# One decoder layer with mLSTM and differential attention: a new hand-written order of steps, norms as steps of their own, and a merge in pairs

## The chip, the cores and the metric

The kernel runs on one core of a Trainium2 chip. The metric is the device time of one execution in microseconds. All matrix products run on the matmul engine (TensorE, PE in the profile); VectorE (DVE), ScalarE (ACT) and GpSimd (POOL) do the rest, and most transfers are issued from SyncE's queue (SP).

## The reference

One layer over 512 tokens of width 1024 in float32:

```python
h = rmsnorm(x, norm_mix_g)
proj = h @ w_in        # mLSTM q,k,v,o,i,f | attention q,k,v | two branch gates
qk = silu(causal_dwconv(concat([mq, mk]), m_conv_w, m_conv_b))     # width 4
hm = mlstm_chunkwise(mq_c, mk_c, mv, i_pre, f_pre)                 # 4 heads x 128
ya = (sigmoid(mo) * head_rmsnorm(hm, m_norm_g)) @ w_br_m
a  = softmax(q1 k1^T/8 + bias) - lam * softmax(q2 k2^T/8 + bias)   # 4 heads, causal
yb = (head_rmsnorm(a @ dv, da_norm_g) * (1 - lam_init)) @ w_br_d
x  = x + (sigmoid(g_a) * ya + sigmoid(g_b) * yb) @ w_out
u  = causal_dwconv(rmsnorm(x, norm_ffn_g) @ w_up, ffn_conv_w, ffn_conv_b)   # width 3
x  = x + (gelu(gate) * value) @ w_down                             # d_ff 2816
x  = x + sigmoid(rmsnorm(x, norm_ple_g) @ w_ple_gate) * (p @ w_ple)
return rmsnorm(x, norm_final_g)
```

## The kernel before

Activations are kept with features on the 128 partitions and the 512 tokens along the free axis, so x is eight tiles of 128x512. To keep float32 accuracy each operand of a product is split into a high and a low part (`split`: ScalarE copies the high part, VectorE subtracts it), and `mm3` (L94) makes three matmuls of each product, on lines 96, 97 and 98; so helpers' lines stand in the profile, and the tile's name says whose step it is. `wload` (L100) brings 128x1024 weights by SP into `raw`, and splits them into `whi` and `wlo`; each of the three has two buffers. One weight tile feeds 24 matmuls of 512 columns.

PSUM has eight banks of 128x512: four under the tag "mm" for projections, two "sc" for scores, sums and transposes, two "acc" for the products of a head (`num` and `den` of an mLSTM head, `av` of an attention head). SBUF tags with few buffers are "ev" (3: `u` and `y` of a convolution, `y` of an attention query or key), "rb" (3), "e" (4), "hn" (4), "qk" (10), "hz" (16), "v" (16: values of both branches, later the mixed chunks) and "x" (8: the branch gates).

The mixing stage is written as a list of steps, `ORDER` (L49). A planner goes through the steps' instructions in this order as priorities and fixes, when the program is built, the sequence of each engine from modelled durations; it draws later steps forward where an earlier one is not ready in its model. Weight loads and their splits have a raised priority. On the chip each engine works through its sequence in order. The steps:

- `mqN`, `mkN` (`conv_silu`, L213): projection, four-tap convolution on VectorE, SiLU by Tanh. The projection's bank is read by one VectorE multiplication (L219).
- `if0`, `ct0`: the gates' projection and their scans on VectorE.
- `mN` (`mlstm`, L409): four score products, weighted products into `num` and `den`.
- `MN` (`mlstm_end`, L432): the sum of squares and the output gate with its projection; `NN` (`mlstm_norm`, L450): the root by Ln and Exp (`rsqrt_of`, L152), which need another table of ScalarE than Tanh, and the split into `hmh`, `hml`.
- `dqN`, `dkN`, `dv0` (L240, L251, L281): attention's queries, keys and values. `dv0` is 96 matmuls into all four "mm" banks at once.
- `bias0`: bias tiles by GpSimd's queue, tied behind the last convolution's memset traced so far.
- `aN` (`attention`, L459): eight score tiles with a softmax each (VectorE adds the bias and takes the maximum, L472; a negation, L475; Exp on ScalarE, L476; a reciprocal, L477; L480 and L481 combine the two halves), transposes (`at`) and the product with the values (`av`).
- `AN` (`attention_end`, L491): square, sum over features, root, split into `hdh`, `hdl`.
- `gaN`, `gbN` (`gate`, L502): branch gates.

After the list comes the merge (L549 to L565), chunk by chunk: chunk j takes one weight tile, whose first half multiplies the four mLSTM heads into `ya` and whose second half the four attention heads into `yb`; the gates' Tanh is tied behind `last_exp`, the Exp of the last norm. The output projection (`wo`), the ConvFFN (`ug`, `uv`, `wd`) and the embedding (`pg`) follow and are untouched.

Of the kernel before, what the change touches and what calls it, by code (L numbers as in the profile page):

```python
# [11 lines left out]
F32 = mybir.dt.float32  # L12
# [34 lines left out]


ORDER = """  # L49
if0 mq0 mk0 mq1 mk1 ct0 m0 m1 mk3 mq2 dk0 M0 M1 mk2 bias0 m2 mq3 M2 m3 dq0 dv0 M3 a0 dk1 dq1  # L50
A0 a1 N0 A1 dk2 dq2 N1 ga3 dq3 a2 N2 A2 ga0 ga2 gb1 dk3 N3 a3 gb3 gb2 gb0 ga1 A3
"""


# [1 line left out]
def trunk_kernel(ctx, tc, xT, pT, par, biasT, lamv, w_if, w_in, w_v, w_br, w_out, w_up,  # L56
# [12 lines left out]
    def rt(tag, name):  # L69
        return big.tile([P, S], F32R, tag=tag, name=name, bufs=NBUF[tag])  # L70
# [76 lines left out]
            nc.scalar.activation(q, src, AF.Square)  # L147
            nc.vector.tensor_add(acc, acc, q)

    last_exp = None  # L150

    def rsqrt_of(r, v, a, before=None):  # L152

        if before is not None:
            with tc.issue_after(before.ins):
                nc.scalar.preload_act_table_set("natural_log_exp_and_others")
        nc.scalar.activation(r, v, AF.Ln, scale=2.0 ** -LN_SHIFT)
        nonlocal last_exp
        last_exp = nc.scalar.activation(r, r, AF.Exp, scale=-0.5, bias=lnb)
        nc.scalar.activation(a, r, AF.Square)  # L160
        nc.vector.scalar_tensor_tensor(a, v, -0.5, a, op0=ALU.mult, op1=ALU.mult)
        nc.vector.scalar_tensor_tensor(r, a, 1.5, r, op0=ALU.add, op1=ALU.mult)
# [293 lines left out]
        return hi, lo  # L456


    def attention(hh, q, k):  # L459
        av = []  # L460
        for i in range(NB):
            n = (i + 1) * P
            nw = max(n, 2 * P)
            es, sums = [], []
            for z in range(2):
                s = ps("sc", f"ds{hh}{i}{z}", nw)
                for b in range(2):
                    nc.tensor.matmul(s, lhsT=q[z][:, i * P:(i + 1) * P], rhs=k[z][b][:, :nw],  # L468
                                     start=b == 0, stop=b == 1)
                e = tt("e" if z == 0 else "rb", f"e{z}", n)  # L470
                mx = tp.tile([P, 4], F32, tag="mx", name="mx", bufs=8)
                nc.vector.tensor_tensor_reduce(  # L472
                    out=e, in0=s[:, :n], in1=bias[hh][:, S - n:], scale=1.0, scalar=-3.0e38,
                    op0=ALU.add, op1=ALU.max, accum_out=mx[:, 0:1])
                nc.vector.tensor_scalar_mul(mx[:, 1:2], mx[:, 0:1], -1.0)  # L475
                nc.scalar.activation(e, e, AF.Exp, bias=mx[:, 1:2], accum_out=mx[:, 2:3])  # L476
                nc.vector.reciprocal(mx[:, 3:4], mx[:, 2:3])  # L477
                es.append(e)
                sums.append(mx[:, 3:4])
            nc.vector.tensor_scalar(es[1], es[1], sums[1], nlam, op0=ALU.mult, op1=ALU.mult)  # L480
            nc.vector.scalar_tensor_tensor(es[0], es[0], sums[0], es[1], op0=ALU.mult, op1=ALU.add)  # L481
            av.append(es[0])
        o = ps("acc", f"av{hh}")
        for j in range(NB):
            tps = ps("sc", f"at{hh}{j}", S - j * P)
            for i in range(j, NB):
                nc.tensor.transpose(tps[:, (i - j) * P:(i - j + 1) * P], av[i][:, j * P:(j + 1) * P], ident)
            weighted("a", j, lambda a, b: split(a, b, tps), dv, hh, (o,))
        return o

    def attention_end(hh, o):  # L491
        y, v, r = tt("hn", "y"), tt("hn", "v"), tt("hn", "r")
        nc.scalar.activation(y, o, AF.Copy, scale=col(C_GD + hh))
        ss, last = mean_square(o, v, f"hd{hh}")
        nc.vector.tensor_scalar(v, ss, 1.0 / P, EPS, op0=ALU.mult, op1=ALU.add)
        rsqrt_of(r, v, ss, None if hh else last)
        nc.vector.tensor_mul(y, y, r)
        hi, lo = rt("hz", f"hdh{hh}"), rt("hz", f"hdl{hh}")
        split(hi, lo, y, 1.0 - LAM_INIT)
        return hi, lo  # L500

    def gate(c, name):  # L502
# [9 lines left out]
    for step in ORDER.split():  # L512
        what, i = step[:-1], int(step[-1])
        if what == "if":
            rd, cols = gates()
        elif what == "ct":
            ct = turn_cols(cols)
        elif what == "mq":
            mq[i] = conv_silu(i, 0.5, f"mq{i}")
        elif what == "mk":  # L520
            mk[i] = conv_silu(4 + i, 0.5 * P ** -0.5, f"mk{i}")
        elif what == "mo":
            mo[i] = out_gate(i)
        elif what == "m":
            sums[i] = mlstm(i)
        elif what == "M":
            hm[i] = mlstm_end(i, *sums[i], mo.get(i))
        elif what == "N":
            hm[i] = mlstm_norm(i, *hm[i])
        elif what == "dv":  # L530
            dv = vproj(1, "dv")
        elif what == "bias":
            bias, nlam = make_bias(), make_nlam()
        elif what == "dq":
            dq[i] = queries(8 + i, f"dq{i}")
        elif what == "dk":
            dk[i] = keys(12 + i, f"dk{i}")
        elif what == "a":
            sums[i] = attention(i, dq[i], dk[i])
        elif what == "A":  # L540
            hd[i] = attention_end(i, sums[i])
        elif what == "ga":
            ga[i] = gate(20 + i, "ga")
        elif what == "gb":
            gb[i] = gate(28 + i, "gb")
    hm, hd = ([t[i] for i in range(H)] for t in (hm, hd))


    mixed = []  # L549
    for j in range(KD):  # L550
        ta = ga[j] if j in ga else gate(20 + j, "ga")
        tb = gb[j] if j in gb else gate(28 + j, "gb")
        with tc.issue_after(last_exp.ins):
            for t in (ta, tb):
                nc.scalar.activation(t, t, AF.Tanh, scale=0.5)
        w = wload(w_br[j])
        oa, ob = ps("mm", "ya"), ps("mm", "yb")
        proj(oa, w, 0, hm)
        proj(ob, w, 4, hd)
        nc.vector.scalar_tensor_tensor(ta, ta, 1.0, oa, op0=ALU.add, op1=ALU.mult)  # L560
        nc.vector.scalar_tensor_tensor(tb, tb, 1.0, ob, op0=ALU.add, op1=ALU.mult)
        nc.vector.tensor_add(ta, ta, tb)
        hi, lo = rt("v", f"mxh{j}"), rt("v", f"mxl{j}")
        split(hi, lo, ta, 0.5)
        mixed.append((hi, lo))  # L565


    x2, h2 = [], []
# [238 lines left out]
def _pack(x, p, rel_bias, norm_mix_g, w_in, b_if, m_conv_w, m_conv_b, m_norm_g, da_lambda, da_norm_g,  # L807
          w_br_m, w_br_d, w_out, norm_ffn_g, w_up, ffn_conv_w, ffn_conv_b, w_down, norm_ple_g,
          w_ple_gate, w_ple, norm_final_g):
    w = w_in[0]  # L810
    mq, mk, mv, mo = (w[:, 512 * i:512 * (i + 1)] for i in range(4))
    gif = np.zeros((D, 64), np.float32)
    gif[:, 0:H] = w[:, 2048:2052]
    gif[:, 32:32 + H] = w[:, 2052:2056]
    dq, dk, dv = (w[:, 2056 + 512 * i:2056 + 512 * (i + 1)] for i in range(3))
    win = np.concatenate([mq, mk, dq, dk, mo, w[:, 3592:]], axis=1)
    wv = np.concatenate([v.reshape(4, 2, P, S).transpose(0, 2, 1, 3).reshape(4, P, 2 * S) for v in (mv, dv)])
    nf = DFF // P
    order = np.stack([nf + np.arange(nf), np.arange(nf)], axis=1).ravel()
    wup = _chunks(w_up[0])[order]  # L820
    par = np.zeros((P, NPAR), np.float32)
    for c, v in ((C_GMIX, norm_mix_g[0]), (C_GFFN, norm_ffn_g[0]), (C_GPLE, norm_ple_g[0]),
                 (C_GM, m_norm_g[0]), (C_GD, da_norm_g[0])):
        v = _cols(v)
        par[:, c:c + v.shape[1]] = v
    mc = np.concatenate([m_conv_w[0], m_conv_b], axis=0)
    par[:, C_MCONV:C_MCONV + 40] = mc.reshape(5, 8, P).transpose(2, 1, 0).reshape(P, 40)
    fc = np.concatenate([ffn_conv_w[0], ffn_conv_b], axis=0)
    par[:, C_FCONV:C_FCONV + 176] = fc.reshape(4, 2 * nf, P)[:, order].transpose(2, 1, 0).reshape(P, 176)
    par[0:H, C_B] = b_if[0, :H]  # L830
    par[32:32 + H, C_B] = b_if[0, H:]
    return {
        "xT": _fmajor(x[0]), "pT": _fmajor(p[0, 0]), "par": par, "biasT": _bias_tiles(rel_bias),
        "lamv": da_lambda[0],
        "w_if": gif.reshape(KD, P, 64).transpose(1, 0, 2).reshape(P, KD * 64), "w_in": _chunks(win), "w_v": wv,
        "w_br": np.concatenate([_chunks(w_br_m[0]), _chunks(w_br_d[0])], axis=2),
        "w_out": _chunks(w_out[0]), "w_up": wup, "w_down": _chunks(w_down[0]),
        "w_gate": w_ple_gate[0].reshape(KD, P, D), "w_ple": w_ple[0].reshape(2, P, 2, S).transpose(2, 1, 0, 3).reshape(2, P, D), "gfin": norm_final_g[None],
    }
# [18 lines left out]
```

## Time and profile before

| | us |
|---|---|
| median of 3 runs | 837.1 (836.33 to 837.5) |
| the profiled execution | 836.26 |
| its span, first to last instruction | 833.3 |

TensorE is busy in nearly the whole span and the other engines are not. Its mean granted clock is 0.992 of full speed. By stage: the value projection of the mLSTM branch to 30 us, the steps of the list to about 273, the merge and the output projection to about 408, the ConvFFN to about 780, the embedding and the last norm to the end. Idle time of another engine costs nothing by itself; what counts is where TensorE waits, for whom, and at which clock it runs.

### The profile page before, as it was taken

Reading aid. Unit: us, or ns where it says so; the run is one execution under the profiler, and the core shown is the slowest. Engines: PE = TensorE matmul, PEld = TensorE weight load, DVE = VectorE, ACT = ScalarE, POOL = GpSimd, SP = SyncE. Lnnn points to the kernel's source line nnn. Section 1 sums busy time; section 2 is a strip of 40 time slices with the busy share of each in tenths; the row PEclk is TensorE's granted clock in tenths of the full one; section 3 lists DMA queues with packets and bytes.
Section 4 is the critical chain, followed back from the end, with each engine's and each line's share of the span. In section 5 each row is a group of like instructions: output and inputs, shape, how many; then the busy total and the mean of one; then the engine's idle time right before and its main releaser. Section 6 shows DMA issues by size and latency. Waiting matters only on the chain.

```text
span 833.3 us, 9859 instructions
## 1 busy us (share of the span) xinstructions
PE 811.2 (97%) x3661; PEld 665.4 (80%) x3661; DVE 539.7 (65%) x873; ACT 397.8 (48%) x614; POOL 27.3 (3%) x111
## 2 busy tenths in 40 slices
PE   8999999999999699999999999999999999999995
PEld 6878878878777588888788888888888888888884
DVE  7689885589977654455677777777777333343545
ACT  6546854487664632334554444444444432232434
POOL 0011200000000000000000000000000000000000
PEclk9999999999999899999999999999999999999998
DMA  6242532212222122252322222223223323333402
GB/s 245 77 131 98 174 115 74 101 51 76 77 77 76 51 101 101 96 187 97 126 102 94 87 97 101 101 102 115 89 99 102 95 89 96 95 112 96 147 31 76
DMA packets 28119, 84.54 MB, mean 101 GB/s; under 512 B 3316, under 2 KB 4992, under 8 KB 28072
## 3 DMA queue, kind: packets, MB, share of 16 engines
q1 hardware_dynamic: 27256, 81.96, 28.9%
q0 software_dynamic: 528, 1.70, 0.7%
q8 instruction: 28, 0.46, 0.2%
q10 hardware_dynamic: 288, 0.27, 0.1%
q14 instruction: 19, 0.16, 0.1%
HBM read 81.79 MB, written 2.13 MB: 101 GB/s over the span
## 4 chain that ended last, share of the span: by engine, by line
PE 81%; ACT 2%; issue 1%; DVE 1%; POOL 0%; POOLq 0%; DVEq 0%; ACTq 0%
PE uv L96 5%; PE wd L98 5%; PE wd L96 5%; PE uv L98 5%; PE uv L97 5%; PE wd L97 5%; PE ug L96 5%; PE ug L98 5%; PE ug L97 5%; PE ga L96 2%; PE ga L98 2%; PE ga L97 2%; PE gb L98 2%; PE gb L97 2%; PE gb L96 2%; PE wo L96 2%
## 5 line engine op out<-in xcount | busy, mean ns | idle before, releaser
L88 ACT CAST whi<-raw 128x1024 fp32r<-128x1024 f32 (+1 forms) x136 | 137.7, 1013 | 221.5 <-issue 72.5
L89 DVE TENSOR_TENSOR wlo<-raw,whi 128x1024 fp32r<-128x1024 f32 (+2 forms) x135 | 159.3, 1180 | 89.5 <-ACT whi L88 88.1
L97 PE MATMUL wd<-gl,whi 128*128 128x512 f32 x176 | 68.5, 389 | 0.0
L98 PE MATMUL wd<-gh,wlo 128*128 128x512 f32 x176 | 68.5, 389 | 0.0
L96 PE MATMUL wd<-gh,whi 128*128 128x512 f32 x176 | 68.5, 389 | 0.0
L592 DVE SCALAR_TENSOR_TENSOR y<-u,prm,y 128x512 f32<-128x512 f32 x88 | 65.6, 749 | 1.5
L88 ACT CAST gh<-y 128x512 fp32r<-128x512 f32 x22 | 13.7, 622 | 55.6 <-DVE y L601 55.6
L587 DVE TENSOR_TENSOR u<-uv,rffn 128x512 f32<-128x512 f32 x22 | 15.2, 692 | 38.1 <-PE uv L98 38.1
L97 PEld LDWEIGHTS wd<-gl,whi 128*128 128x128 f32 x176 | 33.0, 188 | 6.9
L98 PEld LDWEIGHTS wd<-gh,wlo 128*128 128x128 f32 x176 | 33.0, 188 | 6.9
L96 PEld LDWEIGHTS wd<-gh,whi 128*128 128x128 f32 x176 | 33.0, 188 | 6.8
L590 ACT ACTIVATE y<-u,prm 128x512 f32<-128x512 f32 x44 | 35.7, 812 | 0.5 <-DVE u L587 0.3
L599 ACT ACTIVATE y<-y 128x512 f32<-128x512 f32 x22 | 13.9, 632 | 38.7 <-DVE y L592 38.7
L96 PE MATMUL wo<-mxh,whi 128*128 128x512 f32 x64 | 24.9, 389 | 0.0
L97 PE MATMUL wo<-mxl,whi 128*128 128x512 f32 x64 | 24.9, 389 | 0.0
L98 PE MATMUL wo<-mxh,wlo 128*128 128x512 f32 x64 | 24.9, 389 | 0.0
L89 DVE TENSOR_TENSOR gl<-y,gh 128x512 fp32r<-128x512 f32 x22 | 15.2, 692 | 14.7 <-ACT gh L88 14.7
L476 ACT ACTIVATE e<-e,mx 128x128 f32<-128x128 f32 (+3 forms) x32 | 17.8, 556 | 7.8 <-DVE mx L475 7.8
L96 PE MATMUL yb<-hdh,whi 128*128 128x512 f32 x32 | 13.2, 412 | 6.5 <-ACT hdh L91 6.5
L224 DVE SCALAR_TENSOR_TENSOR y<-u,prm,y 128x512 f32<-128x512 f32 x24 | 17.9, 744 | 0.1
L472 DVE CUSTOM_DVE_ANT_0 e<-ds,bias 128x128 f32<-128x128 f32 (+3 forms) x32 | 15.3, 484 | 3.2 <-PE ds L468 3.0
L575 DVE TENSOR_TENSOR x<-x,wo 128x512 f32<-128x512 f32 x8 | 5.5, 688 | 17.2 <-PE wo L98 17.2
(1081 smaller groups left out, 2200.8 us busy)
## 6 DMA issues: line engine op xcount, KB each, us to landing
raw<-in_w_up SPq DMA_DIRECT2D x44, 512.0 KB, 3.2
raw<-in_w_in SPq DMA_DIRECT2D x36, 512.0 KB, 3.2
raw<-in_w_down SPq DMA_DIRECT2D x16, 512.0 KB, 3.5
x<-in_xT SPq DMA_DIRECT2D x16, 256.0 KB, 4.7
raw<-in_w_br SPq DMA_DIRECT2D x8, 512.0 KB, 3.1
raw<-in_w_out SPq DMA_DIRECT2D x8, 512.0 KB, 3.3
raw<-in_w_gate SPq DMA_DIRECT2D x8, 512.0 KB, 3.3
raw<-in_w_down SPq DMA_DIRECT2D x8, 384.0 KB, 3.1
```

Of the source, the lines that this page charges most:

```text
L88: nc.scalar.copy(hi, src)
L89: nc.vector.tensor_sub(lo, src, f(hi))
L96: nc.tensor.matmul(o, lhsT=lh, rhs=rh, start=start, stop=False)
L97: nc.tensor.matmul(o, lhsT=lh, rhs=rl, start=False, stop=False)
L98: nc.tensor.matmul(o, lhsT=ll, rhs=rh, start=False, stop=stop)
L224: nc.vector.scalar_tensor_tensor(y, u[:, i:i + S], col(c0 + i), y, op0=ALU.mult, op1=ALU.add)
L472: nc.vector.tensor_tensor_reduce(out=e, in0=s[:, :n], in1=bias[hh][:, S - n:], scale=1.0, scalar=-3.0e38, op0=ALU.add, op1=ALU.max, accum_ ...
L476: nc.scalar.activation(e, e, AF.Exp, bias=mx[:, 1:2], accum_out=mx[:, 2:3])
L587: nc.vector.tensor_mul(u[:, 2:514], o, rB)
L590: nc.scalar.activation(y, u[:, 2:514], AF.Identity, scale=col(c0 + 2), bias=col(c0 + 3))
L592: nc.vector.scalar_tensor_tensor(y, u[:, i:i + S], col(c0 + i), y, op0=ALU.mult, op1=ALU.add)
L599: nc.scalar.activation(gt, gt, AF.Gelu_apprx_tanh)
```

## The change

- `ORDER` is new: `dv0` directly behind `m0`, `dk0 dq0` and `a0` ahead of mLSTM heads 2 and 3, and the norms grouped (`N0 N1 H0` behind `a1`).
- Attention's norm is a step of its own, `H` (`attention_norm`), with `y` and `v` kept in "hz" tiles; a load of the Ln table is issued behind head 3's sum only.
- The softmax takes the negated score and its minimum, Exp gets a scale of -1, and one reciprocal serves both halves.
- The merge takes chunks in pairs. The weights are packed anew, so that one tile holds one branch of two chunks; `ya` of both, then `yb` of both. `ya` of chunks 2 and 3 goes to "acc" banks. The gates' Tanh is tied behind the last softmax Exp.

```diff
-if0 mq0 mk0 mq1 mk1 ct0 m0 m1 mk3 mq2 dk0 M0 M1 mk2 bias0 m2 mq3 M2 m3 dq0 dv0 M3 a0 dk1 dq1
-A0 a1 N0 A1 dk2 dq2 N1 ga3 dq3 a2 N2 A2 ga0 ga2 gb1 dk3 N3 a3 gb3 gb2 gb0 ga1 A3
+if0 mq0 mk0 mq1 ct0 m0 dv0 mk1 m1 M0 bias0 dk0 dq0 M1 a0 mk2 mq2 A0 m2 mk3 mq3 M2 m3 dk1 dq1 M3 a1 N0 N1 H0 A1
+dk2 dq2 N2 H1 ga3 dq3 a2 N3 A2 H2 ga0 ga2 gb1 dk3 a3 gb3 gb2 gb0 ga1 A3 H3
...
-        last_exp = nc.scalar.activation(r, r, AF.Exp, scale=-0.5, bias=lnb)
+        nc.scalar.activation(r, r, AF.Exp, scale=-0.5, bias=lnb)
...
-                    out=e, in0=s[:, :n], in1=bias[hh][:, S - n:], scale=1.0, scalar=-3.0e38,
-                    op0=ALU.add, op1=ALU.max, accum_out=mx[:, 0:1])
-                nc.vector.tensor_scalar_mul(mx[:, 1:2], mx[:, 0:1], -1.0)
-                nc.scalar.activation(e, e, AF.Exp, bias=mx[:, 1:2], accum_out=mx[:, 2:3])
-                nc.vector.reciprocal(mx[:, 3:4], mx[:, 2:3])
+                    out=e, in0=s[:, :n], in1=bias[hh][:, S - n:], scale=-1.0, scalar=3.0e38,
+                    op0=ALU.add, op1=ALU.min, accum_out=mx[:, z:z + 1])
+                last_softmax = nc.scalar.activation(e, e, AF.Exp, scale=-1.0, bias=mx[:, z:z + 1],
+                                                    accum_out=mx[:, 2 + z:3 + z])
...
+            nc.vector.reciprocal(mx[:, 4:6], mx[:, 2:4])
...
     def attention_end(hh, o):
-        y, v, r = tt("hn", "y"), tt("hn", "v"), tt("hn", "r")
+        y, v = f(rt("hz", f"hdy{hh}")), f(rt("hz", f"hdv{hh}"))
...
-        rsqrt_of(r, v, ss, None if hh else last)
-        nc.vector.tensor_mul(y, y, r)
+        return y, v, last
+
+    def attention_norm(hh, y, v, last):
+        r, t = tt("hn", "r"), tt("hn", "t")
+        rsqrt_of(r, v, t, last if hh == H - 1 else None)
+        nc.vector.tensor_mul(t, y, r)
         hi, lo = rt("hz", f"hdh{hh}"), rt("hz", f"hdl{hh}")
-        split(hi, lo, y, 1.0 - LAM_INIT)
+        split(hi, lo, t, 1.0 - LAM_INIT)
         return hi, lo
...
-    for j in range(KD):
-        ta = ga[j] if j in ga else gate(20 + j, "ga")
-        tb = gb[j] if j in gb else gate(28 + j, "gb")
-        with tc.issue_after(last_exp.ins):
-            for t in (ta, tb):
+    for m in range(0, KD, 2):
+        js = (m, m + 1)
+        gates = [(ga[j] if j in ga else gate(20 + j, "ga"), gb[j] if j in gb else gate(28 + j, "gb")) for j in js]
+        with tc.issue_after(last_softmax.ins):
+            for t in (t for pr in gates for t in pr):
                 nc.scalar.activation(t, t, AF.Tanh, scale=0.5)
-        w = wload(w_br[j])
-        oa, ob = ps("mm", "ya"), ps("mm", "yb")
-        proj(oa, w, 0, hm)
-        proj(ob, w, 4, hd)
...
+        outs = []
+        for n, (tag, ys) in enumerate((("acc" if m == 2 else "mm", hm), ("mm", hd))):
+            w = wload(w_br[m + n])
+            outs.append([ps(tag, ("ya", "yb")[n]) for _ in js])
+            for i in range(2):
+                proj(outs[n][i], w, 4 * i, ys)
+        for i, j in enumerate(js):
+            ta, tb = gates[i]
...
```

## Rows read from the trace of the kernel before

**Rows 1.** The page's busy times: us, share of the span, instructions.

```profile
PE 811.2 (97%) x3661; PEld 665.4 (80%) x3661; DVE 539.7 (65%) x873; ACT 397.8 (48%) x614; POOL 27.3 (3%) x111
```

**Rows 2.** Waits of TensorE: us in total, times, the longest.

```profile
PE yb L96 <- ACT hdh L91: 6.5, 1, 6.5
...
PE s L96 <- ACT mk0h L91: 1.4, 1, 1.4
PE num L96 <- ACT pph L88: 1.1, 2, 0.6
PE av L96 <- ACT aph L88: 0.2, 1, 0.2
```

**Rows 3.** TensorE's timeline at the merge: start, duration, instruction, idle before.

```profile
273.58 0.39 PE L97 MATMUL yb<-hdl,whi 128*128 128x512 f32 x1
273.81 0.39 PE L98 MATMUL yb<-hdh,wlo 128*128 128x512 f32 x1
280.68 0.79 PE L96 MATMUL yb<-hdh,whi 128*128 128x512 f32 x1 [6.48 <-ACT hdh L91]
...
284.84 0.40 PE L98 MATMUL ya<-hmh,wlo 128*128 128x512 f32 x1
```

**Rows 4.** Stretches: length, busy time (instructions) by engine, granted clock, DMA share, GB/s.

```profile
60.00:100.00 40.00, 38.64 (x183) 31.83 (x184) 36.86 (x60) 29.75 (x52) 8.92 (x25) 1.00 0.42 140
...
137.00:153.90 16.90, 16.90 (x76) 14.02 (x75) 5.08 (x6) 5.09 (x7) 0.00 (x0) 1.00 0.26 94
...
160.00:260.00 100.00, 99.70 (x474) 79.65 (x473) 89.83 (x241) 70.50 (x146) 3.38 (x13) 1.00 0.21 74
...
277.80:280.60 2.80, 0.00 (x0) 0.00 (x0) 1.89 (x3) 2.80 (x7) 0.00 (x0) 0.51 0.00 0
```

**Rows 5.** Timelines of VectorE and ScalarE in the same hole, as rows 3.

```profile
272.41 0.69 DVE L495 TENSOR_SCALAR v<-hd3ss 128x512 f32<-128x512 f32 x1 [0.59 <-PE hd3ss L169]
...
277.10 0.69 DVE L161 SCALAR_TENSOR_TENSOR hd3ss<-v,hd3ss 128x512 f32<-128x512 f32 x1
...
279.03 0.68 DVE L497 TENSOR_TENSOR y<-y,r 128x512 f32<-128x512 f32 x1
...
273.14 0.63 ACT L157 ACTIVATE r<-v 128x512 f32<-128x512 f32 x1 [2.04 <-DVE v L495]
273.80 0.72 ACT L159 ACTIVATE r<-r,lnb 128x512 f32<-128x512 f32 x1
274.54 1.28 ACT L555 ACT_TABLE_LOAD   x1
275.84 0.63 ACT L555 ACTIVATE ga<-ga 128x512 f32<-128x512 f32 x1
276.37 0.58 ACT L160 ACTIVATE hd3ss<-r 128x512 f32<-128x512 f32 x1
...
280.01 0.61 ACT L91 ACTIVATE hdh<-y 128x512 fp32r<-128x512 f32 x1
```

**Rows 6.** Timelines of TensorE, VectorE and ScalarE in 49 to 58.

```profile
49.45 0.39 PE L98 MATMUL mq<-h7h,wlo 128*128 128x512 f32 x1
...
54.26 1.23 DVE L89 TENSOR_TENSOR wlo<-raw,whi 128x1024 fp32r<-128x1024 f32 x1 [0.25 <-ACT whi L88]
...
56.66 0.69 DVE L219 TENSOR_TENSOR u<-mq,rmix 128x512 f32<-128x512 f32 x1
...
53.19 1.04 ACT L88 CAST whi<-raw 128x1024 fp32r<-128x1024 f32 x1
```

**Rows 7.** ScalarE's stretch ahead of Ln: length, busy time (instructions), clock, DMA, GB/s.

```profile
260.60:273.10 12.50, 4.35 (x8) 1.00 0.13 43
```

**Rows 8.** VectorE's groups of two lines in 150 to 300: busy us, mean ns | idle before.

```profile
L477 DVE RECIPROCAL mx<-mx 128x1 f32<-128x1 f32 x32 | 4.2, 156 | 0.1
L475 DVE TENSOR_SCALAR mx<-mx 128x1 f32<-128x1 f32 x32 | 4.2, 145 | 0.3
```

**Rows 9.** GpSimd's timeline: three of the four bias loads' issues.

```profile
92.81 1.62 POOL L364 DMA_DIRECT2D bias<-in_biasT  x3 [0.37 <-issue]
```

More of the change, by code (lines that the diff above doesn't have):

```diff
@@ L148, in sumsq_add @@
             nc.vector.tensor_add(acc, acc, q)
-    last_exp = None
     def rsqrt_of(r, v, a, before=None):
@@ L157, in rsqrt_of @@
         nc.scalar.activation(r, v, AF.Ln, scale=2.0 ** -LN_SHIFT)
-        nonlocal last_exp
-        last_exp = nc.scalar.activation(r, r, AF.Exp, scale=-0.5, bias=lnb)
+        nc.scalar.activation(r, r, AF.Exp, scale=-0.5, bias=lnb)
         nc.scalar.activation(a, r, AF.Square)
@@ L456, in mlstm_norm @@
         return hi, lo
+    last_softmax = None
     def attention(hh, q, k):
+        nonlocal last_softmax
         av = []
@@ L463, in attention @@
             nw = max(n, 2 * P)
-            es, sums = [], []
+            es = []
+            mx = tp.tile([P, 6], F32, tag="mx", name="mx", bufs=8)
             for z in range(2):
@@ L470, in attention @@
                 e = tt("e" if z == 0 else "rb", f"e{z}", n)
-                mx = tp.tile([P, 4], F32, tag="mx", name="mx", bufs=8)
                 nc.vector.tensor_tensor_reduce(
-                    out=e, in0=s[:, :n], in1=bias[hh][:, S - n:], scale=1.0, scalar=-3.0e38,
-                    op0=ALU.add, op1=ALU.max, accum_out=mx[:, 0:1])
-                nc.vector.tensor_scalar_mul(mx[:, 1:2], mx[:, 0:1], -1.0)
-                nc.scalar.activation(e, e, AF.Exp, bias=mx[:, 1:2], accum_out=mx[:, 2:3])
-                nc.vector.reciprocal(mx[:, 3:4], mx[:, 2:3])
+                    out=e, in0=s[:, :n], in1=bias[hh][:, S - n:], scale=-1.0, scalar=3.0e38,
+                    op0=ALU.add, op1=ALU.min, accum_out=mx[:, z:z + 1])
+                last_softmax = nc.scalar.activation(e, e, AF.Exp, scale=-1.0, bias=mx[:, z:z + 1],
+                                                    accum_out=mx[:, 2 + z:3 + z])
                 es.append(e)
-                sums.append(mx[:, 3:4])
-            nc.vector.tensor_scalar(es[1], es[1], sums[1], nlam, op0=ALU.mult, op1=ALU.mult)
-            nc.vector.scalar_tensor_tensor(es[0], es[0], sums[0], es[1], op0=ALU.mult, op1=ALU.add)
+            nc.vector.reciprocal(mx[:, 4:6], mx[:, 2:4])
+            nc.vector.tensor_scalar(es[1], es[1], mx[:, 5:6], nlam, op0=ALU.mult, op1=ALU.mult)
+            nc.vector.scalar_tensor_tensor(es[0], es[0], mx[:, 4:5], es[1], op0=ALU.mult, op1=ALU.add)
             av.append(es[0])
@@ L541, in trunk_kernel @@
             hd[i] = attention_end(i, sums[i])
+        elif what == "H":
+            hd[i] = attention_norm(i, *hd[i])
         elif what == "ga":
@@ L549, in trunk_kernel @@
     mixed = []
-    for j in range(KD):
-        ta = ga[j] if j in ga else gate(20 + j, "ga")
-        tb = gb[j] if j in gb else gate(28 + j, "gb")
-        with tc.issue_after(last_exp.ins):
-            for t in (ta, tb):
-                nc.scalar.activation(t, t, AF.Tanh, scale=0.5)
-        w = wload(w_br[j])
-        oa, ob = ps("mm", "ya"), ps("mm", "yb")
-        proj(oa, w, 0, hm)
-        proj(ob, w, 4, hd)
[L560 to L565, printed above, removed]
+    for m in range(0, KD, 2):
[3 more added lines that the diff above has]
+            for t in (t for pr in gates for t in pr):
+                nc.scalar.activation(t, t, AF.Tanh, scale=0.5)
+        outs = []
[6 more added lines that the diff above has]
+            ta, tb = gates[i]
+            nc.vector.scalar_tensor_tensor(ta, ta, 1.0, outs[0][i], op0=ALU.add, op1=ALU.mult)
+            nc.vector.scalar_tensor_tensor(tb, tb, 1.0, outs[1][i], op0=ALU.add, op1=ALU.mult)
+            nc.vector.tensor_add(ta, ta, tb)
+            hi, lo = rt("v", f"mxh{j}"), rt("v", f"mxl{j}")
+            split(hi, lo, ta, 0.5)
+            mixed.append((hi, lo))
     x2, h2 = [], []
@@ L835, in _pack @@
         "w_if": gif.reshape(KD, P, 64).transpose(1, 0, 2).reshape(P, KD * 64), "w_in": _chunks(win), "w_v": wv,
-        "w_br": np.concatenate([_chunks(w_br_m[0]), _chunks(w_br_d[0])], axis=2),
+        "w_br": np.stack([_chunks(v[0]).reshape(4, 2, P, S).transpose(0, 2, 1, 3).reshape(4, P, 2 * S)
+                          for v in (w_br_m, w_br_d)], axis=1).reshape(KD, P, 2 * S),
         "w_out": _chunks(w_out[0]), "w_up": wup, "w_down": _chunks(w_down[0]),
```

## Prediction

> **What bounds the kernel now.** I read the page's busy times first: TensorE is busy for 811.2 of 833.3 us, VectorE for 65% and ScalarE for 48% [rows 1]. So the end is set by the matmuls, and since the change removes and adds no matmul, it can only move time in which TensorE stands still or runs slowly. The second view is therefore TensorE's list of waits, where the reader sees that four kinds of wait carry nearly all idle time between the first projection and the tail: 6.5 us once for `hdh`, 1.4 us once for `mk0h`, 1.1 us in two waits for `pph`, 0.2 us for `aph` [rows 2]. The third is the timeline around the longest. Two neighbouring matmuls start 0.23 us apart at full clock (273.58 and 273.81). After the one at 273.81 the next starts at 280.68, and the one at 284.84 is the first at full pace again [rows 3]. Ten matmuls start from 273.81 up to 284.84 (two of them are shown), which at 0.227 each is 2.3 us; the stretch lasts 11.03 us, so 8.76 us are lost. Of these 2.1 us belong to the clock: it is granted at 0.51 of full speed in 277.8 to 280.6 [rows 4], that is its lower level, 1.2 GHz, after TensorE had stood since 274.0. The nine matmuls that start from 280.68 on take 4.16 us instead of 2.04 [rows 3].
>
> The fourth view is what ScalarE and VectorE did in that hole. It is the norm of attention head 3: `v` on VectorE at 272.41, Ln at 273.14, Exp at 273.80, then a table load of 1.28 us and a tanh of the gates before the Square at 276.37, then three VectorE steps with gate work between them (two of the three stand in the rows), and `hdh` at 280.01, ready at 280.62 [rows 5].
>
> **The change part by part.** *Norm of head 3 and the merge.* The gate tanhs are now tied behind the last softmax exponential instead of the last norm's Exp, so neither their table load nor the first of them has to stand between Exp and Square. The chain from the same start is then: Exp ends at 274.52, Square 0.58, three VectorE steps of 0.69, 0.69 and 0.68 without gate work between, `hdh` 0.61, in sum 277.8 instead of 280.62 [rows 5]: 2.8 us sooner. TensorE's work ran out at 274.04 [rows 3], so 3.8 us of hole remain. The pairing fills it. Before, both branches of chunk j share one weight tile, and with two weight buffers and four "mm" banks, `ya` and three quarters of `yb` of two chunks are all that can run without head 3. Afterwards a weight tile holds one branch of two chunks. The same 42 matmuls can run, and when the first tile is done its buffer takes the third, so that `ya` of chunks 2 and 3 can run as well, in the "acc" banks: 24 matmuls of 0.227, 5.4 us. That is 1.6 us more than the hole. One new seam: the weights of `yb` 2 and 3 need a buffer that is free only after those 24 matmuls. A split costs ScalarE 1.04 us and then VectorE 1.23 [rows 6]; six remaining matmuls of `yb` 0 and 1 (1.36 us) and the two that need only the high part (0.45) cover all but 0.5 us. I take 0.5 here; the bounds are 0 and the whole hole, 3.8. So of 8.76 us I expect 8.3 back.
>
> *Table switches.* The change adds a return to the Ln set, issued ahead of head 3's Ln, and a later one to the tanh set for the remaining gates. ScalarE's part of the first stands in the 2 us before Ln, in which it waits for VectorE's `v`; the eight tanhs, about 0.53 apart (275.84 and 276.37), and their load come to 5.5 us and meet a stretch ahead of Ln in which ScalarE is busy for 4.35 of 12.5 us [rows 5, 7]. I cost both at nothing; without that cover each is 1.28 us on the chain. The trace's load takes 1.28 us and the tanh after it starts 1.30 us after the load did. The Trainium skill, page "ScalarE: Activation LUTs", section "What ACT_TABLE_LOAD costs", puts a switch at some 2.66 us, with a drain beside the load, and asks for all functions of one set before the next, which speaks against this change. By the Trainium skill's price the preload alone would outlast its 2 us by 0.6, still within the 1.6 us spare. The drain isn't seen in the row, and I go by the row.
>
> *Softmax.* 32 negations of 0.145 us and 16 of 32 reciprocals of 0.156 go [rows 8], 7.1 us of VectorE. They lie in 160 to 260, where VectorE is busy for 89.8 of 100 us and TensorE nevertheless for 99.7 [rows 4]. What hides there is worth nothing: 0, at most the 0.2 us of the `aph` wait. The sign trick and the wider `mx` tile cost nothing else.
>
> *Norms as steps of their own.* H0 to H2 issue the same instructions as the ends of A0 to A2, later in the order; their tiles move to "hz", 16 buffers, in which head 3 finds its two last ones only when its own `y` and `v` are read, and those reads come before `hdh` anyway. 0.
>
> *Values' projection and head 0 moved forward.* `dv0` is 96 matmuls, 21.8 us, with next to no vector work: in 137 to 153.9, which is mostly it, VectorE is busy for 5.1 of 16.9 us. It now stands where VectorE is busiest, 36.9 of 40 us in 60 to 100 [rows 4], and head 0 with its softmax goes to the mLSTM heads 2 and 3. That should take the 1.4 us at `mk0h` and some of the 1.1 us at `pph` away. Against it: `dv0` needs all four "mm" banks at once. The projection `mq1` ends at 49.68, but VectorE reads its bank only at 56.66 to 57.35, since it has the gate scans and the convolution of `mq0` to finish. With three banks `dv0` can run 18 matmuls for each of its first two weight tiles, 8.2 us in all, which would just reach that point; but the second tile's split ran at 53.19 to 55.49 here, 1.7 us after the first 18 would be done at 53.8 [rows 6]. I take 1.7 us, and the bounds are 0 and 5.6 (the fourth bank wanted after nine matmuls, at 51.7). Its four weight loads pass those of `mk1` on SP's queue, with the same bytes for each 24 matmuls: 0. The four bias loads on POOL's queue now stand behind `mk1`'s memset, ahead of the masks of m1; three issues take 1.62 us [rows 9], so the four hold these masks by up to 2.2 us with projections of dk0 and dq0 to run meanwhile: 0. Of the small waits that remain (1.1 and 0.2) I assume that as much returns elsewhere around head 0. So this part comes to -1.4 + 1.7 = +0.3.
>
> **The sum.** The profiled execution takes 836.26 us: the span of 833.3 and 2.96 around it. 836.26 - 8.3 + 0.3 = 828.3. The median of the runs, 837.1, lies 0.84 above that execution, so 829.1 for the median.
>
> **The rivals.** (a) *The cover isn't put into the hole.* The order of each engine is fixed when the program is built, from modelled durations; if the 24 matmuls are placed behind head 3's product, 3.8 us of hole stay, about as long as TensorE stood before the clock fell (274.0 to 277.8), so 2.1 us of low clock come with it: 829.1 - 0.5 + 5.9 = 834.5. For it speaks that the same planner left 6.5 us open; against it, that it ran every matmul then possible before that. (b) *The bank of `mq1`.* TensorE stands for 5.6 us at 51.7 and the clock falls: 829.1 - 1.7 + 5.6 + 2.1 = 835.1. (c) *Table switches on the chain.* If the tanh load falls before the splits of head 3's products and the preload before its Ln with nothing hiding them, 2.6 us come on, 1.6 are spare: 830.1. By the Trainium skill's 2.66 for each (the page above) it would be 832.8. (d) *Slower: convolutions queue behind head 0's softmax.* Place: from M1 to m3. A convolution holds two of three "ev" tiles until its split, and a projection behind it holds its bank; at the start this held `mq1`'s bank for 7.7 us [rows 6]. If both later pairs (mk2 mq2, mk3 mq3) meet this behind head 0's eight softmax tiles, and the clock falls each time, it costs 2 x (7.7 + 2.1) = 19.6: 848.7. It decides from 9.7 us on, where 838.8 is reached. For it: VectorE's 92% in 60 to 100, with 1.4 us lost there by TensorE. Against it: in 160 to 260 VectorE was nearly as full with all four softmax heads (their 32 negations lie in that view's stretch) and TensorE lost 0.3 us, because gate projections, which need little of VectorE, were drawn in; and `dv0` gives VectorE time to catch up just ahead.
>
> **How the numbers follow.** Forecast 0.62, (a) 0.10, (b) 0.08, (c) 0.07, (d) 0.08, and 0.05 that the front's waits all go and the seam too: 829.1 - 1.7 - 1.3 - 0.5 = 825.6. A run of this kernel can be told from no change from about 0.2%, 1.7 us: 835.4 and 838.8 are the limits. (a) and (b) lie near the first, and a quarter of their chance goes to "same": faster 0.87, same 0.05, slower 0.08. The range goes from 825.0 (just below that last case) to 836.0, which takes in (a), (b) and (c).
>
> **What would show it.** After: no wait of `yb` for `hdh` above 1 us; granted clock 1.0 through the merge; `ya` matmuls in the "acc" banks between the `hd3ss` sums and the last `yb` of chunk 1; no table load between head 3's Exp and Square; a wait of 1 to 3 us at a `dvp` matmul near 50 to 57. A wait over 4 us anywhere between 30 and 270, or a granted clock below 1 there, would make the prediction wrong.

## The result and the profile after

| | median us | runs | ratio to before |
|---|---|---|---|
| before | 836.72 | 835.06 to 837.5 | |
| changed | 848.8 | 847.7 to 850.24 | 1.0148 (1.0125 to 1.0171) |

The profiled execution of the changed kernel took 847.7 us, its span 845.5. The forecast was 829.1, so the sign was wrong. The page's busy times of the changed kernel:

```profile
PE 813.7 (96%) x3661; PEld 665.0 (79%) x3661; DVE 536.8 (63%) x825; ACT 420.2 (50%) x630; POOL 27.4 (3%) x111
```

Against [rows 1] TensorE has the same number of matmuls, VectorE is busy for 2.9 us less, and ScalarE for 22.4 us more, with 16 instructions more: 420.2 and 630 against 397.8 and 614. No arithmetic was added to ScalarE, and this line is where the search begins. TensorE's largest waits (us in total, times, the longest), of which the two at the start are left out:

```profile
PE ds L469 <- DVE mx L473: 6.6, 2, 6.1
PE ds L469 <- ACT dk3h L256: 2.7, 1, 2.7
PE av L96 <- ACT aph L88: 2.6, 1, 2.6
PE num L96 <- ACT pph L88: 1.6, 2, 1.5
PE hd1ss L165 <- ACT csph L163: 1.5, 1, 1.5
...
PE yb L96 <- ACT hdh L91: 1.3, 1, 1.3
PE hm1ss L165 <- ACT csph L163: 1.1, 1, 1.1
```

The 6.5 us of `yb` for `hdh` [rows 2] have become 1.3. In their place stand new waits of attention's products: 6.6, 2.7, 2.6 and 1.5 us. All but the 2.7 us (at 257 to 260) lie between 180 and 240, as a table of stretches of the changed kernel shows (columns as in rows 4):

```profile
100.00:176.00 76.00, 74.62 (x354) 59.63 (x353) 60.08 (x110) 51.79 (x96) 7.92 (x25) 1.00 0.30 95
...
180.00:200.00 20.00, 18.38 (x85) 14.00 (x84) 14.86 (x39) 19.05 (x34) 0.00 (x0) 1.00 0.18 59
200.00:220.00 20.00, 16.46 (x77) 13.33 (x78) 15.72 (x25) 17.66 (x27) 1.40 (x4) 1.00 0.15 52
220.00:240.00 20.00, 13.93 (x61) 11.35 (x60) 14.63 (x38) 15.90 (x30) 0.00 (x0) 0.83 0.16 54
```

In the first stretch, with head 0 among the mLSTM heads, TensorE loses little. In 180 to 240 it is busy for 48.8 of 60 us, and now VectorE has room while ScalarE is the fullest of the others, 19.05 of 20 us in the first stretch. The last stretch shows the clock as well, 0.83 on the mean: it fell to 0.50 within the 6.1 us wait that begins at 225.9. A sign of being wrong that the prediction had named, a wait over 4 us between 30 and 270, came true. ScalarE's timeline of the changed kernel says what fills that engine (start, duration, instruction):

```profile
178.40 1.28 ACT L155 ACT_TABLE_LOAD   x1
179.69 0.63 ACT L155 ACTIVATE r<-hmv 128x512 f32<-128x512 f32 x1
180.34 1.28 ACT L156 ACT_TABLE_LOAD   x1
181.64 0.72 ACT L156 ACTIVATE r<-r,lnb 128x512 f32<-128x512 f32 x1
...
187.80 1.28 ACT L155 ACT_TABLE_LOAD   x1
189.09 0.63 ACT L155 ACTIVATE r<-hmv 128x512 f32<-128x512 f32 x1
189.74 1.28 ACT L476 ACT_TABLE_LOAD   x1
191.04 0.62 ACT L476 ACTIVATE e<-e,mx 128x384 f32<-128x384 f32 x1
```

L155 is the Ln of a norm, L156 its Exp, L476 a softmax. Each Ln is preceded by a table load and the Exp after it by another; at 189.74 it is a softmax of head 1 that has to load its table back, because the Ln of an mLSTM norm came between its tiles. How such loads reach TensorE is seen at the longest wait, in the timelines of TensorE, ScalarE and VectorE:

```profile
231.98 0.55 PE L469 MATMUL ds<-dk2h,dq 128*128 128x256 f32 x1 [6.07 <-DVE mx L473]
...
224.21 1.28 ACT L155 ACT_TABLE_LOAD   x1
...
226.15 1.28 ACT L156 ACT_TABLE_LOAD   x1
...
228.74 1.03 ACT L88 CAST whi<-raw 128x1024 fp32r<-128x1024 f32 x1
...
229.80 1.23 DVE L89 TENSOR_TENSOR wlo<-raw,whi 128x1024 fp32r<-128x1024 f32 x1 [2.70 <-ACT whi L88]
...
231.54 0.28 DVE L473 CUSTOM_DVE_ANT_0 e<-ds,bias 128x128 f32<-128x128 f32 x1
```

The score product needs a bank that VectorE empties at 231.54; ahead of that, VectorE stands 2.70 us for a weight split, which on ScalarE comes behind a norm with its two loads. All table loads of the changed kernel, by line (count | busy us, mean ns):

```profile
L155 ACT ACT_TABLE_LOAD x8 | 10.3, 1283 | 0.1
L156 ACT ACT_TABLE_LOAD x7 | 9.0, 1283 | 0.1
L154 ACT ACT_TABLE_LOAD x3 | 3.8, 1283 | 0.1
...
L476 ACT ACT_TABLE_LOAD x1 | 1.3, 1283 | 0.0
L563 ACT ACT_TABLE_LOAD x1 | 1.3, 1283 | 0.0
```

With three more at other lines they are 23; the kernel before has 7. The 16 loads more are the 16 instructions more, and at 1.283 us each they are 20.5 us, nearly the whole increase of ScalarE's busy time.

The cause is one expression in the diff. Before, `attention_end` passed `None if hh else last`: a load of the set that holds both Ln and Exp, ahead of head 0's norm. All eight norms and the softmaxes between them lived in that set: in the trace of before, this load

```profile
180.92 1.28 ACT L156 ACT_TABLE_LOAD   x1
```

is followed by none until the one at 274.54 [rows 5], behind the last norm's Exp. Afterwards `attention_norm` passes `last if hh == H - 1 else None`: the load comes for head 3 alone, and seven norms have none. Where no load is written, the trace has one ahead of an activation whose function the current set lacks, and the one ahead of Ln doesn't serve the Exp. The Trainium skill, page "ScalarE: Activation LUTs", section "Table sets: the hidden batching unit", counts Ln followed by Exp as one load, since one set has both. These rows differ, two loads for each such pair, and they decide: it is one load only where the common set was loaded explicitly.

### The profile page after: what moved, and what is told of

It reads as the page before. It is cut to its first block, busy times and chain, and to the rows that moved or that the text cites. A ratio compares the mean times of both kernels' runs of the same rounds, so it can differ in the third digit from the quotient of the medians.

```text
span 845.5 us, 9829 instructions
## 1 busy us (share of the span) xinstructions
PE 813.7 (96%) x3661; PEld 665.0 (79%) x3661; DVE 536.8 (63%) x825; ACT 420.2 (50%) x630; POOL 27.4 (3%) x111
## 4 chain that ended last, share of the span: by engine, by line
PE 69%; ACT 8%; issue 2%; DVE 2%; DMA 0%; POOL 0%; POOLq 0%; DVEq 0%; ACTq 0%
PE wd L98 5%; PE uv L96 5%; PE wd L96 5%; PE uv L98 5%; PE uv L97 5%; PE wd L97 5%; PE ug L96 5%; PE ug L98 5%; PE ug L97 5%; PE gb L98 2%; PE wo L96 2%; PE gb L97 2%; PE gb L96 2%; PE wo L97 2%; PE wo L98 2%
## 5 line engine op out<-in xcount | busy, mean ns | idle before, releaser
L476 ACT ACTIVATE e<-e,mx 128x128 f32<-128x128 f32 (+3 forms) x32 | 17.8, 557 | 8.8 <-DVE mx L473 8.4
L598 POOL MEMSET u<- 128x2 f32 x44 | 4.3, 99 | 373.5 <-DVE y L604 362.0
```

The costliest lines, as they stand in the source:

```text
L476: last_softmax = nc.scalar.activation(e, e, AF.Exp, scale=-1.0, bias=mx[:, z:z + 1], accum_out=mx[:, 2 + z:3 + z])
```

## The experiments

Two theories stood after the first reading. *Table theory*: the loss is the extra table loads on ScalarE. *Order theory*: the loss is the new place of head 0, the values and the norms, and the loads only fall into idle time. All measured ratios below are to runs of before on the same chip; its median was 836.31 us beside e1 to e4 and 835.91 beside e5 to e8.

| run | what it is | median us | ratio (95%) |
|---|---|---|---|
| e1 | changed, Ln and Exp set loaded once for the norms | 832.74 | 0.9957 (0.9936 to 0.9979) |
| e2 | before, its explicit load taken out | 846.22 | 1.0122 (1.0101 to 1.0143) |
| e3 | before, merge in pairs alone | 828.85 | 0.9913 (0.9895 to 0.9930) |
| e4 | changed, order of before, load at heads 0 and 3 | 829.26 | 0.9919 (0.9899 to 0.9939) |
| e5 | e1, no Tanh between head 3's load and its Ln | 831.89 | 0.9956 (0.9943 to 0.9968) |
| e6 | e4 with the edit of e5 | 827.29 | 0.9903 (0.9889 to 0.9916) |
| e7 | e6, values' projection forward | 829.81 | 0.9925 (0.9912 to 0.9939) |
| e8 | before, softmax edit alone | 830.95 | 0.9944 (0.9932 to 0.9957) |

**e1, the loads taken out of the changed kernel.**

```diff
+        last_tanh = nc.scalar.activation(t, t, AF.Tanh, scale=0.5)   # out_gate
...
-        rsqrt_of(r, v, t)                                             # mlstm_norm
+        with tc.issue_after(last_tanh.ins):
+            rsqrt_of(r, v, t, None if hh else last_tanh)
```

> The changed kernel with one edit: the norms of the mLSTM heads stand behind the last output gate's Tanh on ScalarE, and the first of them loads the table set that has both Ln and Exp. The order of steps stays. By the built order this takes ScalarE's table loads from 23 to 11. Table theory (the loss is 12 to 16 extra loads of 1.28 us on a ScalarE that is busy for 17.7 and 19.1 us of 20 in 180 to 220): the waits and low clock of TensorE between 176 and 262, 16.5 us together, go nearly all, so 832 to 835 us against 848.8. Order theory (the loss is the new place of attention head 0 and of the norms, and the loads fall into idle time): 845 to 849, with the waits of ds, av and hd1ss still there.

Measured: 832.74 us, 16.1 less than the changed kernel, for 12 loads fewer. TensorE's waits in it, those of the start left out:

```profile
PE yb L96 <- ACT hdh L91: 1.3, 1, 1.3
PE num L96 <- ACT pph L88: 1.2, 2, 1.0
...
PE dvp L96 <- DVE u L216: 0.6, 2, 0.4
PE ds L473 <- DVE mx L477: 0.4, 1, 0.4
PE dvp L97 <- DVE wlo L89: 0.4, 1, 0.4
PE hm1ss L165 <- ACT csph L163: 0.3, 1, 0.3
PE ds L473 <- ACT dk3h L256: 0.3, 1, 0.3
```

The waits of `ds`, `av` and `hd1ss`, 13.4 us together in the changed kernel, are down to 0.7, with the list of steps unchanged. The edit also ties the norms behind a Tanh, which moves the first of them by some 4 us, and the planner then places some neighbouring instructions of ScalarE and VectorE anew; this run alone doesn't part that from the loads. The table theory holds, and the order theory falls as the main cause.

**e2, the same cause in the other kernel.**

```diff
-        rsqrt_of(r, v, ss, None if hh else last)
+        rsqrt_of(r, v, ss)
```

> The kernel before with one edit: its explicit load of the Ln and Exp table set ahead of attention head 0's norm is taken out. The order of steps stays. By the built order the table loads go from 7 to 17. Table theory: ScalarE, busy for 70.5 of 100 us in 160 to 260, gets 12.8 us more; a part of that reaches TensorE, 840 to 850 us against 836.7. Order theory: 836 to 838, as loads alone are hidden.

Measured: 846.22 us, 9.9 more for 10 loads more, with the list of steps of before (here too the planner places some neighbours of the norms anew). Nine of the ten stand in 160 to 260, one at head 3's norm. Its stretch of 160 to 260 (columns as in rows 4):

```profile
160.00:260.00 100.00, 92.94 (x430) 72.71 (x428) 79.57 (x214) 76.56 (x140) 3.38 (x13) 0.98 0.18 64
```

In [rows 4] the same stretch has TensorE busy for 99.70 us; here 92.94, with ScalarE at 76.56 instead of 70.50. So a mean of 77% on ScalarE does not mean that its loads are hidden: they stand between a score and its Exp, or between two steps of a chain that TensorE's next product needs. A load costs 1.3 us in e1 and 1.0 here, each time together with the new placing of its neighbours.

**e3, the merge in pairs alone**, put into the kernel before, the gates' Tanh still behind the last norm's Exp.

> The kernel before with the paired merge alone (the gates' Tanh still behind the last norm's Exp). If the pairing covers head 3's norm as the prediction worked out: the hole of 6.6 us shrinks by the 5.4 us of the 24 added matmuls, the clock stays high, a seam of 0.5 us: 828 to 831 us. If the planner places the 24 matmuls elsewhere: 834 to 837.

Measured: 828.85 us, 7.5 less. TensorE at the place of the former hole:

```profile
280.06 0.39 PE L98 MATMUL ya<-hmh,wlo 128*128 128x512 f32 x1
281.62 0.50 PE L96 MATMUL yb<-hdh,whi 128*128 128x512 f32 x1 [1.18 <-ACT whi L88]
```

Of 6.48 us [rows 3] 1.18 are left. The `ya` matmuls of chunks 2 and 3 run ahead of head 3's part, as worked out. What remains is a wait for ScalarE's split of the next weights, which stood at 280.54; `hdh`, at 281.48, is waited for no more.

**e4, everything of the change but its order**, with the load at head 0 kept. The steps `H0` to `H3` stand right behind `A0` to `A3`.

```diff
-        rsqrt_of(r, v, t, last if hh == H - 1 else None)
+        rsqrt_of(r, v, t, last if hh in (0, H - 1) else None)
```

> The changed kernel with the order of steps of before (each attention norm right behind its head's end) and the load of the Ln and Exp set ahead of head 0's norm as before, besides that ahead of head 3's; 11 table loads by the built order. Table theory and order theory both expect the loss gone: 827 to 831 us, that is before less the 8 us at the merge. If the loss comes from the norm steps, the softmax edit or the paired merge, it stays: 840 to 849.

Measured: 829.26 us. So neither the paired merge nor the softmax edit nor norms as steps of their own cost anything that shows.

**e5 and e6, no Tanh behind head 3's load.** In the changed kernel, e1 and e4 one late gate's Tanh fell between head 3's explicit load and its Ln. In the changed kernel's ScalarE timeline:

```profile
281.27 1.28 ACT L154 ACT_TABLE_LOAD   x1
...
284.87 1.28 ACT L563 ACT_TABLE_LOAD   x1
286.17 0.63 ACT L563 ACTIVATE ga<-ga 128x512 f32<-128x512 f32 x1
286.81 1.28 ACT L155 ACT_TABLE_LOAD   x1
288.11 0.63 ACT L155 ACTIVATE r<-hdv 128x512 f32<-128x512 f32 x1
288.76 1.28 ACT L156 ACT_TABLE_LOAD   x1
290.05 0.72 ACT L156 ACTIVATE r<-r,lnb 128x512 f32<-128x512 f32 x1
```

The explicit load at 281.27 is wasted and three others follow. The edit, in both kernels:

```diff
+            if i == H - 1:                                            # step "H"
+                with tc.issue_after(last_softmax.ins):
+                    for t in [*gb.values(), *ga.values()]:
+                        tanhs = nc.scalar.activation(t, t, AF.Tanh, scale=0.5)
+                hd[i] = (*hd[i][:2], tanhs)      # head 3's load stands behind the last Tanh
...
-            for t in (t for pr in gates for t in pr):                 # merge
+            for t in (t for pr in gates for t in pr) if m >= 4 else ():
```

> The kernel of e1 with one more edit: the eight gates' Tanhs that are ready early are traced ahead of head 3's norm, and the load of the Ln set stands behind the last of them, so that no Tanh falls between that load and Ln (table loads 11 to 9 by the built order). If two switches on head 3's chain made the 1.3 us wait of yb for hdh that e1 kept: that wait goes, 831 to 832 us against 832.7. If the chain itself is too long for its cover: no change.

> The kernel of e4 (order of before) with the same edit at head 3. The wait of yb for hdh, 1.4 us in e4, goes: 827.5 to 828.5 us against 829.3. Compared with e5 in the same call, it prices the new order without any table switch in the way: if the new order is neutral, as the prediction took it (+0.3 us), the two lie within 1 us; if the front's new waits count, e5 is 2 to 4 us longer.

Measured: e5 831.89 us, 0.85 below e1, and e6 827.29, 2.0 below e4. Each pair was measured beside different runs of before, and as ratios e5 and e1 don't differ (0.9956 and 0.9957) and the intervals of e6 and e4 overlap, so neither gain is clear of noise. What the traces show is that TensorE's list of waits has no `yb` any more in either. e6 is faster than both kernels of this study.

Between e5 and e6, which differ in the order and in which norm has the first explicit load, lie 4.6 us. A part of that is not the order's. The first matmul of the gates (`if`) starts at 31.39 us in the profile of e5 and at 29.20 in that of e6. The difference is TensorE's pace in its first matmuls, of e5 and then of e6:

```profile
6.55 2.05 PE L96 MATMUL mvp<-whi,h0h 128*128 128x512 f32 x4 [0.82 <-DVE whi L272]
```

```profile
6.23 1.17 PE L96 MATMUL mvp<-whi,h0h 128*128 128x512 f32 x4 [0.58 <-ACT h1h L138]
```

In 7 to 10 us TensorE starts 8 matmuls in e5 and 15 in e6, while the granted clock stands at 1.00 in both. The slow start is in the profiles of e4, e5 and e7 (`if` at 31.39 to 31.55) and not in the other seven (29.20 to 29.84); e4 has the order of e6, so it doesn't go with the order. Why it comes is open.

The time from that first matmul to the first one of the output projection (`wo`) leaves it out. Called the stage time here, and taken from one execution of each kernel, it is 330.7 us before, 343.1 changed, 326.3 in e1, 340.9 in e2, 324.0 in e3, 324.1 in e4, 325.4 in e5, 322.5 in e6, 323.5 in e7 and 326.7 in e8; from there to the start of the last matmul it is 462.9 to 463.0 in all ten. By this measure the new order costs 2.9 us (e5 against e6).

**e7, the values' projection forward, alone.**

```diff
-if0 mq0 mk0 mq1 mk1 ct0 m0 m1 mk3 mq2 dk0 M0 M1 mk2 bias0 m2 mq3 M2 m3 dq0 dv0 M3 a0 dk1 dq1
+if0 mq0 mk0 mq1 ct0 m0 dv0 mk1 m1 mk3 mq2 dk0 M0 M1 mk2 bias0 m2 mq3 M2 m3 dq0 M3 a0 dk1 dq1
```

> The kernel of e6 with only the values' projection moved forward to its place in the changed order (behind m0, ahead of mk1); attention head 0 stays late. If the bank of mq1 makes the new order's waits: dvp waits of 1 to 2 us come near 50 to 58 and the 1.4 us at mk0h goes, within 1 us of e6. If moving the values away from attention costs more than that (VectorE has no light stretch left at 137 to 154): 2 to 4 us longer than e6.

Measured: 829.81 us, 2.5 above e6, but with the slow start in its profile; in the stage time 1.0 (323.5 against 322.5). The waits at the values' projection are there, 1.0 us in all:

```profile
58.41 0.40 PE L98 MATMUL dvp<-whi,h2l 128*128 128x512 f32 x1
59.24 0.50 PE L96 MATMUL dvp<-whi,h0h 128*128 128x512 f32 x1 [0.43 <-DVE u L216]
```

The product of the fourth bank (`h0h`, long after the others had gone on to `h2`) waits for VectorE's reading of `mq1`'s bank. The 1.4 us at `mk0h` are gone, as expected. So moving the values makes about one of the 2.9 us, by one execution of each; the rest belongs to head 0's place and the grouped norms together, which no run separates.

**e8, the softmax edit alone**, in the kernel before.

> The kernel before with the softmax edit alone (32 negations and 16 reciprocals fewer, 7.1 us of VectorE). Since TensorE waits for none of it in 160 to 260: 836 to 837 us, no difference. If VectorE were a bound there: 832 to 834.

Measured: 830.95 us, 5.0 less than before (3.9 in the stage time), against an expectation of no difference. TensorE's busy time in 160 to 260 is as before, 99.6 us, so the gain isn't where the edit is. It is at the merge. VectorE's last softmax step of head 3, before and then in e8, and `v` and the first product behind the wait in e8:

```profile
262.87 0.75 DVE L481 SCALAR_TENSOR_TENSOR e<-e,mx,e 128x512 f32<-128x512 f32 x1
```

```profile
258.57 0.75 DVE L481 SCALAR_TENSOR_TENSOR e<-e,mx,e 128x512 f32<-128x512 f32 x1
...
268.15 0.69 DVE L495 TENSOR_SCALAR v<-hd3ss 128x512 f32<-128x512 f32 x1 [0.60 <-PE hd3ss L169]
```

```profile
276.42 0.73 PE L96 MATMUL yb<-hdh,whi 128*128 128x512 f32 x2 [1.73 <-ACT hdh L91]
```

The softmax of head 3 ends 4.3 us sooner, `v` comes at 268.15 instead of 272.41 [rows 5], and the wait for `hdh` shrinks from 6.48 to 1.73 us. The clock falls all the same (0.50 in 278 to 280), so its 2.1 us are not part of the gain. TensorE had other work to do in 160 to 260 and lost nothing there; but the same chain, some microseconds earlier, met more of that other work at its end.

## Why the prediction was wrong

*What bounds the kernel.* Right: the matmuls are the same, `wo` and all behind it take the same 463 us in every profile. The differences are waits of TensorE and its clock in the mixing stage, besides its pace in the first matmuls.

*Table switches: the step that failed.* The prediction counted two switches as added and cost them at nothing. The trace shows 16 more loads. It read the diff's new argument as a load added at head 3 and overlooked that the same line removes the load at head 0, on which the seven other norms rested; and so "H0 to H2 issue the same instructions as the ends of A0 to A2" was wrong by the loads put ahead of each Ln and Exp. Taking 12 of them out gives 16.1 us back (e1), and ten put into the kernel before cost 9.9 (e2). Rival (c) had the mechanism, but for the two switches at head 3 only, and said 1.0 for them: e5 against e1 gives 0.9 in the stage time, which the medians don't clear of noise.

*Norm of head 3 and the merge.* Right in mechanism: 8.3 us back forecast, 7.5 measured for the pairing alone (e3; 6.7 in the stage time), and 8.6 with the softmax edit and no switch on the chain (e6; 8.2 in the stage time). In the changed kernel the wait is 1.3 us. The seam was sized at 0.5 us; in e3 it made 1.18, with the gates' Tanhs on ScalarE just ahead of the split, and in e6 no wait is left.

*Softmax: 0 forecast, 5.0 us measured alone (e8).* This term was mis-sized as well: it was sized by the stage in which the instructions stand. Its time came back at the end of the chain to which they belong. Its gain overlaps with that of the pairing, since both fill the same hole: 7.5 and 5.0 alone, 7.1 (e4) to 8.6 (e6) together.

*Values and head 0 forward: +0.3 us forecast.* The wait at the fourth bank is the one described, but smaller (1.7 us taken; in e5 the waits at `dvp` are 0.39 us for weights and 0.43 for the bank). But small waits elsewhere don't cancel: with the grouped norms it is 2.9 us in the stage time; the 4.6 of the medians may hold the slow start of e5's profile besides.

*Rival (d)* gave 848.7 us, next to the measured 848.8, by luck: it is nevertheless wrong. Its place was M1 to m3; there, in 100 to 176, TensorE is busy for 74.6 of 76 us. The loss lies behind it, on another engine.

The sum in the stage time: 322.5 in e6; the new order 2.9 more, e5; two switches ahead of head 3's norm 0.9 more, e1; twelve loads at the other norms 16.8 more, 343.1 in the changed kernel. Against before that is 12.4 us longer, and 12.1 by the medians.

## What to carry to other kernels

Engine state that one instruction sets up for many others, such as the function table, is a part of each of them: when a diff moves or narrows the instruction that sets it, count every later user that now has to set it again. Where two functions share a set, load that set explicitly ahead of the first, keep functions of the other set out of the stretch, and count the table loads of the built program. And time saved on an engine that hides behind another can still pay, at the point where its chain ends in a hole.

## What the runs showed of the hardware

Ln followed by Exp makes two table loads of 1.283 us where the common set isn't loaded explicitly, and a load costs 1.29 to 1.30 us until the next activation starts (178.40 to 179.69, 284.87 to 286.17); no further drain stands beside it in these rows. In e2, where ScalarE's busy share in 160 to 260 goes from 71 to 77%, ten loads more, nine of them there, cost 9.9 us of their own 12.8, so little of them was hidden. At the start, TensorE's first matmuls run at about half the pace in three of the ten profiles (the first four take 2.05 us in e5 and 1.17 in e6) with the granted clock at 1.00 in all, which makes the first 30 us some 2 us longer.
